# Two convolutions inside a recurrent block: ScalarE's taps given to VectorE and GpSimd, four accumulators instead of two

## The chip, the cores and the metric

The kernel runs on one core of a Trainium2 chip. The metric is device time in microseconds, the median of several runs.

## The reference

Two blocks of a network are computed on 256 tokens of width 1024, two layers each, batch 1, all in float32. The first block is the one that matters here. A layer projects the normed input `x` (and a context `ctx` of 256 tokens) to 2848 columns. The first 1024 go to a convolution branch: `val * sigmoid(gate)` gives 512 channels, and each channel is convolved along the 256 tokens with its own 31 weights, a bias is added, then a group norm over groups of 64 channels and SiLU follow:

```
def conformer_conv(u, conv_w, conv_b, cnorm_g, cnorm_b):
    val, gate = jnp.split(u, 2, axis=-1)
    z = val * jax.nn.sigmoid(gate)
    z = dwconv(z, conv_w) + conv_b
    z = group_norm(z, CONV_GROUPS, cnorm_g, cnorm_b, LN_EPS)
    return jax.nn.silu(z)
```

The other columns feed a recurrence (RWKV) over 8 heads of 64, forward and backward in time. Both branches are concatenated and projected; a gated feed-forward follows. The second layer of the context needs the recurrence alone. The second block (another mixer and four feed-forwards) has no such convolution.

## The kernel before

Activations lie with 128 features on the partitions and the 256 tokens along the free axis; 512 channels are four such tiles. Weights come from memory on SyncE's queue as tiles of 128 x 1024 (`raw`, four buffers); ScalarE makes a rounded high part `wh` (line 341) and VectorE the remainder `wl` (line 342), and TensorE does three products for each.

**The stages.** `first` (line 1412) runs four recurrences: on `ctx` of layer 0 ("wide", until some 330 us), on `x` of layer 0 ("half", from some 395 us on, beside the feed-forward of `ctx`), on `ctx` of layer 1 ("all", its inverse at some 840 to 910 us), and on `x` of layer 1 ("wide", some 1080 to 1350 us). A recurrence in chunks of 64 tokens needs the inverse of 32 x 32 triangular blocks (`inverse`, line 944): 31 steps of a product (962) and a difference (964) on VectorE, two block transpositions (967, 969), products on TensorE, and the assembly of two tiles `Q` of 128 x 1024. Each `Q` is set to zero on GpSimd (987), filled in part by copies on ScalarE and VectorE (995), and finished with negated products (1009 on ScalarE, 1011 on VectorE). Then `reads` (1014, masks at 1029), `values` (1041, masks at 1065) and `chain` (1075), which carries the state through four chunks in either direction, alternate TensorE with ScalarE and VectorE.

**The filler of a wide stage.** While the recurrence runs, other work is laid between: `conv_in` (line 659; the product with the sigmoid at 670 gives `z`), and the steps of `ada_steps` (478), which turn 512 KB tiles into modulation vectors through a copy on ScalarE (497, tile `T2b`). In the first wide stage the filler begins with loading and norming `x` (`then_x`, 1454), in both versions.

**The convolution** (`conv`, line 700) is traced behind the recurrence of a wide stage (1443), for each tile `f` of four in turn. The tap in the middle and the taps nearest to it are VectorE's: one instruction (726) multiplies the shifted `z` by its weight and adds to an accumulator `av` (tile `T1c`, two buffers), which 719 begins, behind the last step of the inverse by an explicit order. The farthest taps are GpSimd's: a product (732) into a buffer `tap` (two of them) and an addition (733) into the output `zc`, which 720 sets to zero. Those in between are ScalarE's: it makes the product (730) in the same two buffers, and GpSimd adds it. `NPOOL` and `NPOOLE` (line 38) give, for the first and second wide stage, how many of the 30 outer taps GpSimd and ScalarE take: 10 and 3, then 9 and 3, so VectorE keeps 17, then 18. Last, 737 on VectorE adds `av`, the bias and `zc`. A third convolution (`x` of layer 0, `NPOOLC`) has all taps on GpSimd, behind the first one in its queue, from about 244 to 541 us. Each ends in `group_norm` (745), whose squares also lie in `T1c`.

**The order.** The framework writes the order of each engine's instructions before the run, from the order of tracing as priority and a planned duration for each instruction; on the chip every engine follows its list, and an instruction that waits holds back all behind it. The convolution is traced last in its stage, so its taps are planned into times at which an engine has nothing earlier to do.

Of the kernel before, what the change touches and what calls it, by code (L numbers as in the profile page):

```python
# [12 lines left out]
ALU = mybir.AluOpType  # L13
# [21 lines left out]

NLAST = 2, 4

NPOOL, NPOOLE, NPOOLC = (10, 3), (9, 3), (30, 0)
NTAP = 2

QC, EVERY = (1,), 2
# [217 lines left out]
class Prog:  # L259
# [427 lines left out]
    def mixed_in(self, conv, y, perm=False):  # L687

        mix = self.mixtiles()
        for f in range(NF):  # L690
            src = (conv if f < 4 else y)[:, f % 4, :]
            if perm:
                t = self.T1([P, T])
                a, b = self.unperm(t, src, True)
                self.nc.gpsimd.tensor_copy(a, b)
                src = t
            self.split(src, *mix[f])
        return mix

    def conv(self, l, z, acc, npool, hold=False):  # L700


        nc = self.nc
        o = COLS[f"convw{l}"][0]
        taps = sorted((j for j in range(31) if j != 15), key=lambda j: abs(j - 15))
        nv, na = 30 - npool[0] - npool[1], npool[1]
        parts = [("v", taps[:nv]), ("a", taps[nv : nv + na]), ("p", taps[nv + na :])]

        order = []
        for k, js in parts:  # L710
            order += [((i + 0.5) / len(js), k, j) for i, j in enumerate(js)]
        order.sort()
        zc = [acc[:, f, :] for f in range(4)]
        for f in range(4):
            w = lambda j: self.cols[:, o + 4 * j + f : o + 4 * j + f + 1]
            av = self.T1([P, T]) if nv else None
            if nv:
                with self.tc.issue_after(self.inverted.ins):
                    nc.vector.tensor_scalar(av, z[:, f, :], w(15), None, ALU.mult)
                nc.gpsimd.memset(zc[f], 0.0)  # L720
            else:
                nc.gpsimd.tensor_scalar(zc[f], z[:, f, :], w(15), None, ALU.mult)
            for i, (_, k, j) in enumerate(order):
                d, s = slice(max(0, 15 - j), min(T, T + 15 - j)), slice(max(0, j - 15), min(T, T + j - 15))
                if k == "v":
                    nc.vector.scalar_tensor_tensor(av[:, d], z[:, f, s], w(j), av[:, d], ALU.mult, ALU.add)  # L726
                else:
                    t = self.t(self.pool, [P, T], "tap", bufs=NTAP)
                    if k == "a":
                        nc.scalar.mul(t[:, d], z[:, f, s], w(j))  # L730
                    else:
                        nc.gpsimd.tensor_scalar(t[:, d], z[:, f, s], w(j), None, ALU.mult)  # L732
                    nc.gpsimd.tensor_add(zc[f][:, d], zc[f][:, d], t[:, d])  # L733
                if i % 5 == 4:
                    yield
            if nv:
                nc.vector.scalar_tensor_tensor(zc[f], av, self.col(f"convb{l}", f), zc[f], ALU.add, ALU.add)
            else:
                nc.gpsimd.tensor_scalar(zc[f], zc[f], self.col(f"convb{l}", f), None, ALU.add)
            yield  # L740
        while hold and not self.go:
            yield
        self.group_norm(zc, f"cng{l}", f"cnb{l}", LN_EPS, AF.Silu)
# [200 lines left out]
    def inverse(self, Ld, Lo):  # L944

        nc = self.nc
        fl = lambda t: t.rearrange("p d a c x -> p (d a c) x")  # L950
        Ld, Lo = fl(Ld), fl(Lo)
        tj = self.S([P, 32, 32])
        nc.vector.transpose(tj.rearrange("p r c -> p c r"), Ld.rearrange("p j c -> p c j"))
        X = self.S([P, 32, 32])
        nc.gpsimd.memset(X, 0.0)
        xf = X.rearrange("p r c -> p (r c)")
        nc.gpsimd.memset(xf[:, 0:1024:33], 1.0)
        for k in range(31):
            m = 31 - k
            tmp = self.T1([P, 256])  # L960
            tv = tmp[:, 0 : m * (k + 1)].rearrange("p (a b) -> p a b", b=k + 1)
            nc.vector.tensor_mul(tv, tj[:, k + 1 : 32, k : k + 1].broadcast_to([P, m, k + 1]),  # L962
                                 X[:, k : k + 1, 0 : k + 1].broadcast_to([P, m, k + 1]))
            self.inverted = nc.vector.tensor_sub(X[:, k + 1 : 32, 0 : k + 1], X[:, k + 1 : 32, 0 : k + 1], tv)  # L964
        yield
        qt = self.S([P, 32, 32])
        nc.vector.transpose(qt, X)
        qc = self.S([P, 32, 32])
        nc.vector.transpose(qc, X.rearrange("p r c -> p c r"))

        zss = []
        for d in range(2):
            pz = self.ps((P, 16, 32))
            zs = Lo[:, 16 * d : 16 * d + 16, :]
            for j in range(16):
                J = 16 * d + j
                for h in range(2):
                    r = slice(64 * h + 32, 64 * h + 64)
                    w = slice(64 * h, 64 * h + 32)
                    self.mm(pz[w, j, :], Lo[r, J, :], qt[r, :, J], tile_position=(64 * h + 32, 64 * h))  # L980
            for h in range(2):
                w = slice(64 * h, 64 * h + 32)
                (nc.scalar.copy if h else nc.vector.tensor_copy)(zs[w], pz[w])
            zss.append(zs)
        Q = [self.S([P, 16, CH]) for _ in range(2)]
        for d in range(2):
            nc.gpsimd.memset(Q[d], 0.0)
            js = slice(16 * d, 16 * d + 16)
            src, zs = (qt, qc)[d], zss[d]
            po = self.ps((P, 16, 32))  # L990
            for q in range(4):
                s = slice(32 * q, 32 * q + 32)
                o = (q % 2) * 32
                dst, v = Q[d][s, :, o : o + 32], src[s][:, :, js].rearrange("p c j -> p j c")
                (nc.vector.tensor_copy if q % 2 else nc.scalar.copy)(dst, v)
            for j in range(16):
                J = 16 * d + j
                for h in range(2):
                    w = slice(64 * h, 64 * h + 32)
                    r = slice(64 * h + 32, 64 * h + 64)  # L1000
                    if d == 0:
                        self.mm(po[w, j, :], qc[w, :, J], zs[w, j, :], tile_position=(64 * h, 64 * h))
                    else:
                        self.mm(po[r, j, :], zs[w, j, :], qc[w, :, J], tile_position=(64 * h, 64 * h + 32))
            for h in range(2):
                w = slice(64 * h + 32 * d, 64 * h + 32 * d + 32)
                dst = Q[d][w, :, 32 * (1 - d) : 32 * (1 - d) + 32]
                if h:
                    nc.scalar.mul(dst, po[w], -1.0)
                else:  # L1010
                    nc.vector.tensor_scalar(dst, po[w], -1.0, None, ALU.mult)
        self.Q = Q
# [399 lines left out]
    def first(self):  # L1412
# [41 lines left out]
        def then_x():  # L1454

            zt = lambda: self.t(self.pool, [P, D], "z", bufs=2)
            early.append(self.norm1(0, self.load("x", [zt(), zt()]), 0, False, self.Sr, keep=True))
            yield
            early.append(z())
            mods, conv = self.ada_steps(0, (2, 3, 4, 5)), self.conv_in(0, *early)  # L1460
            for i, _ in enumerate(mods):
                yield
                if i % 4 == 1:
                    next(conv, None)
                    yield
            yield from conv
# [103 lines left out]

TAGS1 = {
    ("Sb", "t"): ("Sb", 2), ("S", "r"): ("S", NS), ("S", "t"): ("S", NS), ("S", "b"): ("Sb", 2),
# [3 lines left out]
    ("tiny", "r"): ("tn", 6), ("tiny", "b"): ("tnb", 4), ("tiny", "c"): ("tnc", 2),  # L1576
}
# [63 lines left out]
```

## Time and profile before

| | us |
|---|---|
| median of 3 runs | 2794.75 |
| lowest and highest | 2785.89, 2794.93 |
| the profiled execution, its own time | 2795.86 |
| its span, first to last instruction | 2794.10 |

The profile is of one execution. Its busy times and waits add up to its span, 1.76 us less than that execution took. Engines: PE is TensorE's matmul, PEld its weight load, DVE VectorE, ACT ScalarE, POOL GpSimd. A row of groups gives line, engine, operation, output and input, shape, count, busy time and mean of one, then the idle time before them and who ended it.

### The profile page before, as it was taken

The page shows a single profiled execution, that of the slowest core. Times are in us where ns is not written, and L with a number is a line of the kernel's source. Part 1 is how long each engine was busy: PE and PEld are TensorE (multiplying, and loading weights), DVE is VectorE, ACT ScalarE, POOL GpSimd, SP SyncE. Part 2 cuts the span into 40 slices and gives each one's busy share as a digit, 9 for nine tenths or more (in the row PEclk, how much of TensorE's full clock was granted, in tenths as well). Part 3 has the DMA queues.
Part 4 walks back from the last instruction along what each step waited for, and adds up shares of the span by engine and source line. Part 5 has one row for each costly group of instructions (what it writes and reads, how often), then busy time and mean ns, then how long its engine had stood idle before and what let it go on. Part 6 is the DMA issues. An engine that isn't in the chain of part 4 may idle for free.

```text
span 2794.1 us, 53718 instructions
## 1 busy us (share of the span) xinstructions
PE 2640.2 (94%) x22398; PEld 2307.3 (83%) x22398; DVE 1728.3 (62%) x2735; ACT 1318.7 (47%) x2007; POOL 613.7 (22%) x609
## 2 busy tenths in 40 slices
PE   7879988999989998989899899999999999999998
PEld 4867777888668897866699899889899898889897
DVE  3894678744578555895555655665655655755655
ACT  5532454433565346532544544554444544644543
POOL 0288899700130001391200000010000000100000
PEclk8978999999999999978899999999999999999999
DMA  7325433433423354234255555524555554525653
GB/s 249 103 75 186 163 129 129 152 135 131 166 76 107 123 180 159 94 127 170 101 186 184 200 187 184 193 91 149 176 188 184 186 184 166 177 90 181 203 184 118
DMA packets 118768, 430.71 MB, mean 154 GB/s; under 512 B 13174, under 2 KB 13686, under 8 KB 118524
## 3 DMA queue, kind: packets, MB, share of 16 engines
q1 hardware_dynamic: 118524, 427.28, 43.9%
q8 instruction: 175, 2.87, 0.4%
q14 instruction: 69, 0.57, 0.1%
HBM read 425.13 MB, written 2.10 MB: 153 GB/s over the span
## 4 chain that ended last, share of the span: by engine, by line
PE 78%; DVE 13%; ACT 4%; issue 2%; DMA 2%; POOL 1%; SPq 0%; ACTq 0%; DVEq 0%; POOLq 0%
PE pb L333 33%; PE acc L333 24%; PE ps L333 19%; DVE wl L342 2%; DVE T1c L726 2%; DVE S L964 1%; DVE T L962 1%; DMA raw<-in_ada 1%; ACT wh L341 1%; POOL tap L732 1%; DVE acc L619 0%; PE acc L438 0%; DVE x L620 0%; DMA raw<-in_wr 0%; DVE S L851 0%
## 5 line engine op out<-in xcount | busy, mean ns | idle before, releaser
L342 DVE TENSOR_TENSOR wl<-raw,wh 128x1024 fp32r<-128x1024 f32 (+1 forms) x654 | 809.7, 1241 | 628.6 <-ACT wh L341 395.1
L341 ACT CAST wh<-raw 128x1024 fp32r<-128x1024 f32 (+1 forms) x654 | 681.7, 1046 | 901.1 <-PE pb L333 343.7
L333 PE MATMUL pb<-xf,wh 128*128 128x256 f32 (+1 forms) x2560 | 489.7, 289 | 14.7 <-DVE T1b L588 4.3
L333 PE MATMUL pb<-S,wh 128*128 128x256 f32 x2560 | 496.4, 291 | 4.3 <-DVE S L630 2.6
L333 PEld LDWEIGHTS pb<-xf,wh 128*128 128x128 f32 (+1 forms) x2560 | 411.6, 195 | 29.7 <-DVE T1b L588 8.1
L333 PEld LDWEIGHTS pb<-S,wh 128*128 128x128 f32 x2560 | 413.4, 194 | 22.0 <-issue 9.8
L333 PE MATMUL ps<-S,wh 128*128 128x256 f32 x2048 | 392.4, 288 | 0.9 <-ACT S L460 0.8
L333 PE MATMUL pb<-xf,wl 128*128 128x256 f32 (+1 forms) x1280 | 371.8, 291 | 1.5 <-DVE wl L342 1.4
L333 PE MATMUL pb<-S,wl 128*128 128x256 f32 x1280 | 370.2, 289 | 0.4 <-DVE wl L342 0.4
L365 POOL TENSOR_TENSOR wl<-raw,wh 128x1024 fp32r<-128x1024 f32 x22 | 52.0, 2374 | 1392.7 <-ACT wh L364 1000.8
L333 PEld LDWEIGHTS ps<-S,wh 128*128 128x128 f32 x2048 | 328.4, 193 | 9.7 <-issue 3.4
L333 PE MATMUL ps<-S,wl 128*128 128x256 f32 x1024 | 294.1, 287 | 1.8 <-DVE wl L342 1.8
L333 PEld LDWEIGHTS pb<-xf,wl 128*128 128x128 f32 (+1 forms) x1280 | 249.0, 194 | 8.0 <-DVE wl L342 2.9
L333 PEld LDWEIGHTS pb<-S,wl 128*128 128x128 f32 x1280 | 248.6, 194 | 5.2 <-issue 3.3
L333 PE MATMUL acc<-wh,T 128*128 128x512 f32 x704 | 206.3, 393 | 0.0
L333 PEld LDWEIGHTS ps<-S,wl 128*128 128x128 f32 x1024 | 197.3, 193 | 3.8 <-DVE wl L342 2.0
L333 PE MATMUL acc<-wh,T1b 128*128 128x512 f32 x528 | 159.0, 399 | 3.5 <-ACT T1b L341 3.5
L333 PEld LDWEIGHTS acc<-wh,T 128*128 128x128 f32 x704 | 127.0, 189 | 23.6
L732 POOL TENSOR_SCALAR tap<-z,cols 128x255 f32<-128x255 f32 (+14 forms) x120 | 138.2, 1161 | 0.0
L333 PEld LDWEIGHTS acc<-wh,T1b 128*128 128x128 f32 x528 | 95.1, 190 | 22.4 <-ACT T1b L341 4.4
L333 PE MATMUL acc<-wl,T 128*128 128x512 f32 x352 | 113.2, 395 | 0.0
L733 POOL TENSOR_TENSOR z<-z,tap 128x255 f32<-128x255 f32 (+14 forms) x120 | 110.4, 920 | 4.1
(444 smaller groups left out, 3949.4 us busy)
## 6 DMA issues: line engine op xcount, KB each, us to landing
raw<-in_fu SPq DMA_DIRECT2D x132, 512.0 KB, 3.2
raw<-in_ada SPq DMA_DIRECT2D x96, 512.0 KB, 4.2
raw<-in_pu SPq DMA_DIRECT2D x88, 512.0 KB, 4.3
raw<-in_qu SPq DMA_DIRECT2D x88, 512.0 KB, 4.0
raw<-in_fd SPq DMA_DIRECT2D x66, 512.0 KB, 3.2
raw<-in_wr SPq DMA_DIRECT2D x51, 512.0 KB, 4.2
raw<-in_pd SPq DMA_DIRECT2D x44, 512.0 KB, 4.3
raw<-in_qd SPq DMA_DIRECT2D x44, 512.0 KB, 3.3
```

The costliest lines, as they stand in the source:

```text
L333: return self.nc.tensor.matmul(out, lhsT, rhs, start=start, stop=stop, **kw)
L341: self.nc.scalar.copy(hi, src)
L342: self.nc.vector.tensor_sub(lo, src, hi.bitcast(F32))
L365: self.nc.gpsimd.tensor_sub(lo, r, hi.bitcast(F32))
L726: nc.vector.scalar_tensor_tensor(av[:, d], z[:, f, s], w(j), av[:, d], ALU.mult, ALU.add)
L732: nc.gpsimd.tensor_scalar(t[:, d], z[:, f, s], w(j), None, ALU.mult)
L733: nc.gpsimd.tensor_add(zc[f][:, d], zc[f][:, d], t[:, d])
L962: nc.vector.tensor_mul(tv, tj[:, k + 1 : 32, k : k + 1].broadcast_to([P, m, k + 1]), X[:, k : k + 1, 0 : k + 1].broadcast_to([P, m, k + 1]))
L964: self.inverted = nc.vector.tensor_sub(X[:, k + 1 : 32, 0 : k + 1], X[:, k + 1 : 32, 0 : k + 1], tv)
```

## The change

The counts of taps become 11 for GpSimd and 0 for ScalarE in both wide stages, so VectorE has 19. The bias is added where the accumulator begins (719), and the accumulator is added to GpSimd's sum by GpSimd (line 737's place). `T1c` has four buffers instead of two, and `T2b` one instead of two. The zeros of `Q` in `inverse`, in all four recurrences, are written by VectorE.

```diff
--- before.py
+++ after.py
@@ -35,7 +35,7 @@
 
 NLAST = 2, 4
 
-NPOOL, NPOOLE, NPOOLC = (10, 3), (9, 3), (30, 0)
+NPOOL, NPOOLE, NPOOLC = (11, 0), (11, 0), (30, 0)
 NTAP = 2
 
 QC, EVERY = (1,), 2
@@ -716,7 +716,7 @@
             av = self.T1([P, T]) if nv else None
             if nv:
                 with self.tc.issue_after(self.inverted.ins):
-                    nc.vector.tensor_scalar(av, z[:, f, :], w(15), None, ALU.mult)
+                    nc.vector.tensor_scalar(av, z[:, f, :], w(15), self.col(f"convb{l}", f), ALU.mult, ALU.add)
                 nc.gpsimd.memset(zc[f], 0.0)
             else:
                 nc.gpsimd.tensor_scalar(zc[f], z[:, f, :], w(15), None, ALU.mult)
@@ -734,7 +734,7 @@
                 if i % 5 == 4:
                     yield
             if nv:
-                nc.vector.scalar_tensor_tensor(zc[f], av, self.col(f"convb{l}", f), zc[f], ALU.add, ALU.add)
+                nc.gpsimd.tensor_add(zc[f], zc[f], av)
             else:
                 nc.gpsimd.tensor_scalar(zc[f], zc[f], self.col(f"convb{l}", f), None, ALU.add)
             yield
@@ -984,7 +984,7 @@
             zss.append(zs)
         Q = [self.S([P, 16, CH]) for _ in range(2)]
         for d in range(2):
-            nc.gpsimd.memset(Q[d], 0.0)
+            nc.vector.memset(Q[d], 0.0)
             js = slice(16 * d, 16 * d + 16)
             src, zs = (qt, qc)[d], zss[d]
             po = self.ps((P, 16, 32))
@@ -1570,8 +1570,8 @@
 
 TAGS1 = {
     ("Sb", "t"): ("Sb", 2), ("S", "r"): ("S", NS), ("S", "t"): ("S", NS), ("S", "b"): ("Sb", 2),
-    ("T1", "r"): ("T1", 4), ("T1", "b"): ("T1b", 6), ("T1", "c"): ("T1c", 2),
-    ("T2", "r"): ("T2", 3), ("T2", "t"): ("T2", 3), ("T2", "b"): ("T2b", 2),
+    ("T1", "r"): ("T1", 4), ("T1", "b"): ("T1b", 6), ("T1", "c"): ("T1c", 4),
+    ("T2", "r"): ("T2", 3), ("T2", "t"): ("T2", 3), ("T2", "b"): ("T2b", 1),
     ("tD", "r"): ("tD", 2), ("tD", "b"): ("tDb", 2),
     ("tiny", "r"): ("tn", 6), ("tiny", "b"): ("tnb", 4), ("tiny", "c"): ("tnc", 2),
 }
```

## Rows read from the trace of the kernel before

**Rows 1.** The page, part 1: busy time of each engine over the span.
```profile
PE 2640.2 (94%) x22398; PEld 2307.3 (83%) x22398; DVE 1728.3 (62%) x2735; ACT 1318.7 (47%) x2007; POOL 613.7 (22%) x609
```

**Rows 2.** Busy time by stretch; columns: stretch, its us, busy (x instructions), PEclk, DMA.
```profile
164.00:228.00 64.00, 54.25 (x692) 44.48 (x692) 60.35 (x122) 23.93 (x44) 53.11 (x53) 0.61 0.23 83
228.00:290.00 62.00, 61.19 (x732) 44.13 (x731) 21.77 (x43) 14.93 (x26) 53.45 (x62) 0.93 0.66 233
1208.00:1268.00 60.00, 48.80 (x616) 35.19 (x616) 59.04 (x113) 17.67 (x30) 53.66 (x57) 0.63 0.33 123
1268.00:1333.00 65.00, 64.55 (x823) 42.29 (x820) 29.50 (x76) 18.97 (x37) 2.46 (x4) 0.92 0.43 155
```

**Rows 3.** Chain of waits, 1100 to 1350 us; columns: start, us, what.
```profile
1245.24 6.73 DVE T1c L726 x11
```

**Rows 4.** Groups by line, VectorE, 164 to 229 us; busy and mean ns, then idle before.
```profile
L726 DVE SCALAR_TENSOR_TENSOR T1c<-x,cols,T1c 128x255 f32<-128x255 f32 (+8 forms) x68 | 35.1, 558 | 0.2
L719 DVE TENSOR_SCALAR T1c<-x,cols 128x256 f32<-128x256 f32 x4 | 2.1, 576 | 0.0
L737 DVE SCALAR_TENSOR_TENSOR x<-T1c,cols,x 128x256 f32<-128x256 f32 x3 | 2.0, 691 | 0.0
```

**Rows 5.** Groups by line, VectorE, 1208 to 1268 us.
```profile
L726 DVE SCALAR_TENSOR_TENSOR T1c<-x,cols,T1c 128x255 f32<-128x255 f32 (+8 forms) x72 | 41.3, 628 | 0.1
L737 DVE SCALAR_TENSOR_TENSOR x<-T1c,cols,x 128x256 f32<-128x256 f32 x3 | 1.4, 466 | 0.0
```

**Rows 6.** Page, part 5: the weight split on VectorE.
```profile
L342 DVE TENSOR_TENSOR wl<-raw,wh 128x1024 fp32r<-128x1024 f32 (+1 forms) x654 | 809.7, 1241 | 628.6 <-ACT wh L341 395.1
```

**Rows 7.** Timeline of VectorE, first wide stage; columns: start, us, then what.
```profile
166.53 1.23 DVE L967 STREAM_TRANSPOSE S<-S 128x1024 f32<-128x1024 f32 x1
182.91 2.23 DVE L726 SCALAR_TENSOR_TENSOR T1c<-x,cols,T1c 128x252 f32<-128x252 f32 x5
186.84 2.09 DVE L995 COPY S<-S 32x512 f32<-32x512 f32 x2 [1.69 <-POOL S L987]
197.09 0.68 DVE L1011 TENSOR_SCALAR S<-ps 32x512 f32<-32x512 f32 x1
200.87 1.53 DVE L737 SCALAR_TENSOR_TENSOR x<-T1c,cols,x 128x256 f32<-128x256 f32 x2
```

**Rows 8.** Timeline of VectorE, second wide stage.
```profile
1215.65 1.23 DVE L967 STREAM_TRANSPOSE S<-S 128x1024 f32<-128x1024 f32 x1
1227.99 2.37 DVE L726 SCALAR_TENSOR_TENSOR T1c<-x,cols,T1c 128x250 f32<-128x250 f32 x4
1241.10 0.68 DVE L1011 TENSOR_SCALAR S<-acc 32x512 f32<-32x512 f32 x1
```

**Rows 9.** Groups by line, GpSimd, 164 to 229 us.
```profile
L732 POOL TENSOR_SCALAR tap<-x,cols 128x243 f32<-128x243 f32 (+4 forms) x21 | 27.0, 1294 | 0.0
L733 POOL TENSOR_TENSOR x<-x,tap 128x244 f32<-128x244 f32 (+6 forms) x28 | 24.3, 867 | 8.8 <-ACT tap L730 7.5
```

**Rows 10.** Groups by line, ScalarE, whole span.
```profile
L730 ACT ACTIVATE tap<-x,cols 128x246 f32<-128x246 f32 (+2 forms) x24 | 12.0, 502 | 41.4 <-POOL x L733 39.2 <-DVE x L670 2.2
L497 ACT COPY T2b<-pb 128x512 f32<-128x512 f32 x20 | 11.7, 584 | 31.5 <-PE pb L333 31.3
```

**Rows 11.** Busy time by stretch, around the third inverse.
```profile
510.00:545.00 35.00, 34.36 (x506) 32.07 (x506) 23.23 (x32) 17.02 (x22) 33.35 (x34) 0.85 0.38 125
```

**Rows 12.** Timeline of VectorE, the inverse beside the feed-forward.
```profile
509.93 1.23 DVE L967 STREAM_TRANSPOSE S<-S 128x1024 f32<-128x1024 f32 x1
524.56 0.68 DVE L1011 TENSOR_SCALAR S<-ps 32x512 f32<-32x512 f32 x1 [0.93 <-PE ps L333]
```

**Rows 13.** Timeline of GpSimd: first tap, and a later idle time.
```profile
133.57 1.86 POOL L732 TENSOR_SCALAR tap<-x,cols 128x245 f32<-128x245 f32 x2 [24.37 <-DVE x L670]
...
272.69 0.93 POOL L722 TENSOR_SCALAR z<-z,cols 128x256 f32<-128x256 f32 x1 [3.38 <-DVE z L670]
```

**Rows 14.** Timeline of VectorE, where it waits for GpSimd.
```profile
455.21 0.42 DVE L962 TENSOR_TENSOR T<-S,S 128x31 f32<-128x31 f32 x1 [3.14 <-POOL S L957]
```

## The prediction

> **What bounds the kernel now.** I began with the busy time of each engine. TensorE is busy for 94% of the span [rows 1], so a change to the vector engines counts only where TensorE waits. The next view, busy time in equal slices, sent me to the two wide stages, and busy time by stretch shows them side by side. From the end of each inverse, VectorE is full, 60.4 of 64 us and 59.0 of 60, while TensorE's granted clock is 0.61 and 0.63 and ScalarE is busy for 23.9 and 17.7 us. Right behind, VectorE is down to 21.8 of 62 and 29.5 of 65 us, TensorE is full and its clock 0.92 to 0.93 [rows 2]. The chain of waits in the second stretch goes through VectorE's taps, 6.7 us of them in one piece [rows 3]. So in two stretches, 124 us together, the time is the sum of VectorE's list, and the taps fill 35.1 and 41.3 us of it [rows 4, 5]. Elsewhere TensorE decides. The view to settle the sum in is therefore VectorE's groups in these stretches.
>
> **The change, part by part.** A term is positive where it makes the kernel longer.
>
> *Taps.* VectorE goes from 17 to 19 per tile in the first wide stage (8 more) and from 18 to 19 in the second (4 more). One takes 35.1/68 = 0.516 us and 41.3/72 = 0.574 us of VectorE [rows 4, 5]: 8 x 0.516 = 4.1 and 4 x 0.574 = 2.3, **+6.4**.
>
> *Sums.* VectorE's last additions go to GpSimd; three of four lay in each stretch, 2.0 and 1.4 us [rows 4, 5]: **-3.4**. The fourth of each lies behind the stretch, where VectorE has room. The bias moves into an instruction that is there anyway: 0.
>
> *Four accumulators.* 719 never stands idle waiting for its buffer: 0.0 [rows 4]. Two at a time already keep VectorE full, so 0 here.
>
> *Zeros of Q.* The trace has no zeroing on VectorE. From below, 719 covers a quarter of the width in 2.1/4 = 0.53 us [rows 4]; from above, the weight split covers the same 128 x 1024 with two inputs in 1.24 us [rows 6]. I take 1.1, near the row of the same shape; four fall into the two stretches, **+4.4** (2.1 to 5.0).
> The Trainium skill (VectorE: DVE Perf Modes, Zero memsets can be issued as uint32) has a memset at one cycle per element whatever the type; an estimate from that, 1024 elements at VectorE's 0.96 GHz, is 1.07 us, and no row here shows it. With it the term would be 4.3.
>
> *The wait for the zeros.* At 186.84 us VectorE stands idle for 1.69 us until GpSimd has zeroed Q behind its own taps [rows 7]: **-1.7**. Ahead of that copy VectorE's list has five taps, 2.23 us, and four, 2.37 us, in the second wide stage [rows 7, 8]; I read them as put there because Q was not ready. With the zeros in VectorE's own list the copy can follow the transpositions, and these taps run later, at best where VectorE has room. That is worth 0 to -4.6; I take **-4.6**, since the stretch behind is 60% idle on VectorE [rows 2].
>
> *GpSimd without ScalarE's taps.* In the first stretch GpSimd waits 7.5 us for ScalarE's products [rows 9]. This is now work, and it slows VectorE: where GpSimd is busy for 53.7 of 60 us instead of 53.1 of 64 [rows 2], a tap costs 0.574 - 0.516 = 0.058 more. For the 7.5/0.516 = 15 taps beside it that is **+0.9** (0 to 1.8).
> The Trainium skill (SBUF — State Buffer, Who interferes with whom) says more: VectorE with two inputs in SBUF and GpSimd reading it exclude each other for a whole instruction, while ScalarE has ports of its own. That rule speaks against the change: 24 products leave the port that nobody shares. Taken whole, each of the 12 new taps on VectorE could wait a full GpSimd addition of 24.3/28 = 0.87 us [rows 9], 10.4 us in place of the 6.4 above, and the sum would be +6.0. The rows agree in direction alone: taps cost more where GpSimd is busier.
>
> *ScalarE.* It loses 24 products, 12.0 us, and 39.2 us of standing still for GpSimd's buffers [rows 10]. I cost this at 0, the striking number of the page notwithstanding: behind it work waits, but VectorE's list is full at the same time. The most it can give is what VectorE is idle in the stretches beyond the 1.7 counted, 3.65 + 0.96 - 1.7 = 2.9 [rows 2]. If VectorE's cover went, ScalarE's waits would come next.
>
> *The other two inverses.* Four zeros there too, at 0: beside the feed-forward TensorE is busy for 34.4 of 35 us [rows 11]. Without that cover, 4 x 1.24 = 5.0 more; 0 to gain, as nothing of TensorE's idle time is there to win beyond 0.6.
>
> *T2b with one buffer.* The 20 copies wait for TensorE's products, 31.3 us, not for a buffer [rows 10]. TensorE reads a copy before it makes what the next one waits for, so 0; no gain is possible.
>
> *GpSimd's list.* No DMA is issued in what moves, and SyncE's queue is passed by nothing. On GpSimd the two wide stages have 23 and 21 tap instructions per tile before, 22 and 22 after and one sum. The sum waits for VectorE, and behind it stand the taps of the next tiles and the third convolution; this is the second rival.
>
> Sum: 6.4 - 3.4 + 4.4 - 1.7 - 4.6 + 0.9 = **+2.0 us**. The profiled execution took 2795.86 us (span 2794.10 and 1.76 around it), 1.1 above the median shown; against the median I forecast 2794.75 + 2.0 = **2796.8 us**. With all bounds one way: no taps displaced +4.6, zeros +0.6, other inverses +5.0, port +0.9, together 2808; the other way zeros -2.3, ScalarE -2.9, port -0.9, inverses -0.6, together 2790. I count 0.5%, 14 us, as what a measurement can tell from no change, so this case lies within it.
>
> **Rivals.** *The inverse's tail gets free (faster).* From the first transposition to the last negated product it takes 166.53 to 197.77, 31.2 us, and 1215.65 to 1241.78, 26.1 us, with taps between [rows 7, 8]; beside the feed-forward, without taps, 509.93 to 525.24, 15.3 us [rows 12]. If Q that is ready sooner takes not nine taps but most of them out of these tails, and they end behind the stretch, half of the excess is 7.9 + 5.4 = 13.3 us and the whole 26.7; I put this case at -20, **2777 us**. For it: low clock and idle TensorE beside a full VectorE [rows 2]. Against it: taps put off still have to run, and the masks that the recurrence waits for stand in the same list. It decides where more than some 25 taps (25 x 0.55 = 14 us) leave the stretches.
>
> *GpSimd waits for VectorE at the sum (slower).* GpSimd begins at 133.57 us [rows 13]; with 11 products and 11 additions and the sum, a tile takes 11 x 1.29 + 12 x 0.87 = 24.6 us [rows 9], so two are through at 183. VectorE ends the first two accumulators at about 200.87 us [rows 7]. If the list has the sums right behind each tile's taps, GpSimd stands still for some 18 us; with four accumulators in turn, longer. A lag of 3.4 us is lost again where GpSimd waits for z of the third convolution [rows 13]; the rest stays, as that convolution alone has 4 x 30 x 2 = 240 instructions for GpSimd, and in the "half" stage VectorE already waits 3.1 us for GpSimd's zeros of the inverse [rows 14]. So 18 - 3.4, about 15 us: **2812 us**. Against it: GpSimd gains 7.5 us in the same place, and a planned order may put the sums later. It decides when GpSimd's lag at the end of the first wide stage is over 3.4 us.
>
> *The change does little of what it says.* Accumulators that nobody waited for and a ScalarE that nobody waited for would leave the time as it is: that is inside the forecast, at 2795.
>
> **How the numbers follow.** The forecast's case, all terms small, 0.52, with its own range 2790 to 2808. The free tail 0.27: the engine lists are written anew, and 124 us of half-used TensorE is much to win. GpSimd's wait 0.21. The range reaches from 2771, into most of the first rival, to 2816, just past the second. Faster by over 0.5% takes the first rival alone, slower the second.
>
> **What would show it.** Right: VectorE still full in both stretches, their length within 4 us, 76 taps in each at 0.5 to 0.6 us, zeros at about 1.1 us followed at once by the copies, ScalarE without the 39 us and no shorter stage for it. First rival: taps seen behind the stretch, tails under 25 us. Second: GpSimd idle at its sums until VectorE is done, and the waits at the "half" inverse grown. Wrong altogether: a difference of over 10 us in a part without convolution or inverse.

## The result, and the profile after

The changed kernel takes **2805.98 us**, the median of 5 runs (2800.15 to 2811.6), against 2794.39 for the kernel before in the same comparison, 11.6 us more. The ratio over all executions is **1.0052**, 95% interval 1.0029 to 1.0075, half a per cent longer. That lies at the edge of what the prediction called no change, inside the range of its likeliest case. The profiled execution took 2805.98 us with a span of 2804.2, 10.1 us more than before.

The page's busy times of the changed kernel hardly differ from before [rows 1]:

```profile
PE 2641.4 (94%) x22398; PEld 2304.8 (82%) x22398; DVE 1731.0 (62%) x2747; ACT 1309.6 (47%) x1983; POOL 614.5 (22%) x609
```

The busy time by stretch, with the bounds of [rows 2]:

```profile
164.00:228.00 64.00, 52.83 (x661) 42.83 (x661) 63.28 (x124) 21.68 (x38) 59.96 (x56) 0.63 0.22 83
228.00:290.00 62.00, 59.01 (x662) 42.09 (x662) 21.47 (x42) 12.76 (x22) 49.25 (x59) 0.89 0.59 206
1208.00:1268.00 60.00, 53.81 (x616) 33.57 (x615) 55.29 (x114) 15.08 (x24) 53.33 (x55) 0.69 0.34 121
1268.00:1333.00 65.00, 58.30 (x842) 40.32 (x842) 30.07 (x78) 15.62 (x32) 14.40 (x18) 0.92 0.51 182
```

VectorE (the third busy time) is fuller in the first taps' stretch, but in the second it now stands idle for 4.7 of 60 us, where it was full. Its groups, first stretch (164 to 234 us), to be read against [rows 4]:

```profile
L726 DVE SCALAR_TENSOR_TENSOR T1c<-x,cols,T1c 128x255 f32<-128x255 f32 (+9 forms) x76 | 42.1, 599 | 0.1
L987 DVE MEMSET S<- 128x1024 f32 x2 | 1.8, 912 | 0.3 <-issue 0.2 <-DVE T1c L726 0.2
```

And in the second (1208 to 1275 us), against [rows 5]:

```profile
L726 DVE SCALAR_TENSOR_TENSOR T1c<-x,cols,T1c 128x255 f32<-128x255 f32 (+9 forms) x76 | 37.4, 544 | 0.1
L987 DVE MEMSET S<- 128x1024 f32 x2 | 1.8, 912 | 0.3 <-DVE T1c L726 0.2 <-issue 0.2
```

So 76 taps in each, 0.554 and 0.492 us of VectorE apiece, and zeros whose records last 0.91 us. Where the zeros stand shows in the timeline of VectorE in the second wide stage (start, us, then what):

```profile
1220.11 1.23 DVE L967 STREAM_TRANSPOSE S<-S 128x1024 f32<-128x1024 f32 x1
...
1236.05 0.42 DVE L1065 TENSOR_TENSOR T<-acc,const 64x256 f32<-64x256 f32 x1 [1.71 <-PE acc L333]
1236.39 1.94 DVE L969 STREAM_TRANSPOSE S<-S 128x1024 f32<-128x1024 f32 x1
...
1240.10 0.91 DVE L987 MEMSET S<- 128x1024 f32 x1 [0.16 <-DVE T1c L726]
1240.94 1.52 DVE L726 SCALAR_TENSOR_TENSOR T1c<-x,cols,T1c 128x252 f32<-128x252 f32 x4
1242.49 2.01 DVE L995 COPY S<-S 32x512 f32<-32x512 f32 x2
...
1255.23 0.68 DVE L1011 TENSOR_SCALAR S<-acc 32x512 f32<-32x512 f32 x1
```

The inverse's tail, from 967 to the end of the last 1011, is 35.8 us, before 26.1 [rows 8]. Four taps stand between a zero and the copies that need it, and VectorE waits for TensorE in the middle of it.

**Where the time went.** I cut both executions at the transposition of `Ld` (953) that opens a wide stage, and at the first product with the gate (619) behind it:

| stretch | before | after | difference |
|---|---|---|---|
| start to 953 of the first wide stage | 110.9 | 113.9 | +3.0 |
| first wide stage, 953 to 619 | 287.2 | 291.2 | +4.0 |
| to 953 of the second | 762.8 | 761.6 | -1.2 |
| second wide stage, 953 to 619 | 201.6 | 207.4 | +5.8 |
| the rest of the span | 1431.5 | 1430.1 | -1.4 |

The first line is no effect of the change: up to there both programs have the same order of instructions. Each column is one execution: two more executions with the list of the kernel before (in part 2 below, where only the second stage differs) took 763.4 and 757.1 us where 762.8 stands here, so a difference of a few us in one line is not shown by it. The second wide stage, cut at 953, 967, the last 1011, the group norm of the recurrence (385) and 619, looks so before and after (columns as in [rows 2]):

```profile
1160.94:1215.65 54.71, 48.33 (x534) 39.58 (x533) 52.55 (x109) 18.92 (x32) 35.11 (x37) 0.95 0.35 126
1215.65:1241.78 26.13, 25.70 (x403) 19.28 (x403) 25.36 (x48) 11.15 (x17) 21.07 (x21) 0.63 0.39 142
1241.78:1326.16 84.38, 76.07 (x988) 52.48 (x984) 50.96 (x116) 22.06 (x42) 26.28 (x29) 0.83 0.41 151
1326.16:1362.58 36.42, 35.87 (x133) 24.18 (x133) 21.28 (x35) 16.23 (x26) 10.51 (x12) 0.91 0.26 93
```

```profile
1166.67:1220.11 53.44, 43.36 (x513) 38.08 (x513) 50.96 (x105) 16.39 (x26) 33.28 (x35) 0.96 0.33 120
1220.11:1255.91 35.80, 35.80 (x428) 21.61 (x430) 31.49 (x60) 10.40 (x15) 35.17 (x34) 0.69 0.31 108
1255.91:1335.92 80.01, 73.31 (x983) 50.15 (x981) 43.28 (x110) 20.15 (x38) 20.60 (x25) 0.87 0.45 164
1335.92:1374.12 38.20, 37.32 (x133) 25.37 (x133) 20.36 (x35) 16.12 (x26) 7.39 (x12) 0.87 0.26 86
```

The tail grew by 9.7 us and what is behind it lost 4.4. TensorE (first busy time) has no gap in the tail at all, at a granted clock of 0.69, between its levels of 1.2 (0.5) and 2.4 GHz (1.0), and does 428 products there instead of 403.

The prediction read the chain of waits in one piece [rows 3]. By line, over the whole second wide stage, before and after, it is:

```profile
by line: PE acc L333 29.9%; PE pb L333 15.4%; DVE T1c L726 12.3%; PE ps L333 6.5%; DVE S L964 5.5%; DVE T L962 5.2%; DVE wl L342 5.2%; issue 2.9%; DVE S L1029 2.4%; DMA raw<-in_ada 2.1%; DVE T L1065 1.3%; DVE S L953 1.1%; ACT S L995 1.0%; D
```

```profile
by line: PE acc L333 34.7%; PE pb L333 18.5%; PE ps L333 7.8%; DVE T L962 5.4%; DVE wl L342 5.2%; DVE S L964 4.9%; DVE T1c L726 3.8%; DMA raw<-in_ada 2.9%; issue 2.7%; DVE S L1029 2.3%; DMA raw<-in_wo 1.6%; PE acc L1052 1.4%; DVE S L953 1.1
```

VectorE's taps (`DVE T1c L726`) hold 12.3% of 201.6 us, 24.8, before and 3.8% of 207.4, 7.9, after; TensorE's products (`PE`) took their place. In the first wide stage it went the other way, 7.4% of 287.2 us, 21.3, before and 12.2% of 291.2, 35.5, after:

```profile
by line: PE pb L333 36.9%; PE acc L333 16.2%; DVE T1c L726 7.4%; PE ps L333 6.7%; DVE T L962 3.5%; DVE wl L342 3.3%; POOL tap L732 3.3%; DVE S L964 3.2%; issue 2.6%; DMA raw<-in_wc 1.8%; POOL x L733 1.5%; DMA z<-in_x 1.4%; DVE S L995 1.3%; 
```

```profile
by line: PE pb L333 35.3%; PE acc L333 16.3%; DVE T1c L726 12.2%; PE ps L333 7.5%; DVE wl L342 3.9%; DVE T L962 2.9%; issue 2.5%; DVE S L964 2.5%; DVE T L1065 1.6%; DMA raw<-in_wc 1.5%; DMA z<-in_x 1.3%; DVE S L995 1.1%; DVE xf L342 1.0%; D
```

### The profile page after: what moved, and what is told of

It reads as the page before. It is cut to its first block, busy times and chain, and to the rows that moved or that the text cites. A ratio compares the mean times of both kernels' runs of the same rounds, so it can differ in the third digit from the quotient of the medians.

```text
span 2804.2 us, 53671 instructions
## 1 busy us (share of the span) xinstructions
PE 2641.4 (94%) x22398; PEld 2304.8 (82%) x22398; DVE 1731.0 (62%) x2747; ACT 1309.6 (47%) x1983; POOL 614.5 (22%) x609
## 4 chain that ended last, share of the span: by engine, by line
PE 78%; DVE 14%; ACT 4%; DMA 2%; issue 2%; POOL 0%; SPq 0%; ACTq 0%; DVEq 0%; POOLq 0%
PE pb L333 33%; PE acc L333 25%; PE ps L333 19%; DVE wl L342 3%; DVE T1c L726 2%; DVE T L962 1%; DVE S L964 1%; PE acc L438 1%; DMA raw<-in_ada 1%; ACT wh L341 1%; DVE acc L619 0%; DMA raw<-in_wr 0%; DVE x L620 0%; DVE tDb L519 0%; ACT L384 0%
## 5 line engine op out<-in xcount | busy, mean ns | idle before, releaser
L732 POOL TENSOR_SCALAR tap<-x,cols 128x245 f32<-128x245 f32 (+5 forms) x88 | 101.0, 1158 | 46.8 <-DVE x L670 46.8
```

## The experiments

The theories: **load**, the one of the prediction (the time is VectorE's work in the two stretches); **tail**, in the first expectations called order theory (taps that stand between transposition and last negated product make the tail long); **GpSimd** (sums wait for VectorE); and, formed after the first four runs, **filler** (the modulation steps: the 64 products with `csil` on 32 loads of 512 KB that TensorE's list spreads over the second wide stage).

**1. Undo one part, or move the taps.** Zeros back on GpSimd:

```diff
-            nc.vector.memset(Q[d], 0.0)
+            nc.gpsimd.memset(Q[d], 0.0)
```

> The changed kernel with the zeros of Q back on GpSimd. Load theory (what counts is how much work VectorE's list has in the two stretches): four zeros of 0.91 us leave the stretches, 2806 - 3.6 = 2802 us. Order theory (what counts is how many taps the planned order puts between the first transposition and the last negated product of a wide inverse): the list has 27 and 35 taps there, the changed kernel's 29 and 36, so 3 x 0.55 = 1.7 less, 2804 us. GpSimd theory (sums wait for VectorE): 2806 us, or more, since GpSimd gets four zeros behind its taps again. The three lie close together; what tells is the tail of the second inverse: 35 us or more by the order theory, under 33 by the load theory.

Two accumulators and two `T2b` again:

```diff
-    ("T1", "r"): ("T1", 4), ("T1", "b"): ("T1b", 6), ("T1", "c"): ("T1c", 4),
-    ("T2", "r"): ("T2", 3), ("T2", "t"): ("T2", 3), ("T2", "b"): ("T2b", 1),
+    ("T1", "r"): ("T1", 4), ("T1", "b"): ("T1b", 6), ("T1", "c"): ("T1c", 2),
+    ("T2", "r"): ("T2", 3), ("T2", "t"): ("T2", 3), ("T2", "b"): ("T2b", 2),
```

> The changed kernel with two accumulators T1c (and two T2b) as before; taps, sums and zeros stay as changed. Load theory: VectorE has the same work, 2805 to 2807 us. Order theory: the list has 19 and 28 taps between the first transposition and the last negated product in place of 29 and 36, 18 fewer: 18 x 0.55 = 10 us less, 2796 us, and the second tail some 31 us in place of 35.8. GpSimd theory: with two accumulators the sums of the first two tiles come earlier, a few us less, 2802 us, with the tail as long as it is.

The kernel before with line 987 alone changed:

```diff
-            nc.gpsimd.memset(Q[d], 0.0)
+            nc.vector.memset(Q[d], 0.0)
```

> The kernel before with only the zeros of Q moved to VectorE. Load theory: 4 x 0.91 us more in the stretches, less the wait of 1.69 us for GpSimd: 2794.4 + 2 = 2796.5 us. Order theory: the list has 23 and 21 taps in the tails, the kernel before 28 and 27: 11 fewer, 6 us less, 2788 us or a little more for the zeros, 2790; both tails under 30 and 26 us.

The changed kernel with no tap in a tail (719 is ordered behind what `self.inverted` names):

```diff
-                    nc.vector.tensor_scalar(dst, po[w], -1.0, None, ALU.mult)
+                    self.inverted = nc.vector.tensor_scalar(dst, po[w], -1.0, None, ALU.mult)
```

> The changed kernel with the accumulators' begin ordered behind the last negated product of the inverse, so that no tap stands in the two tails. Load theory: the same work in another order, and VectorE's taps still have to end before the group norm: 2804 to 2808 us. Order theory: the tails of 32.0 and 35.8 us fall to some 17 us each (15.3 beside the feed-forward, without taps); the taps run in the stretch behind, where VectorE is idle for some 40 and 35 us and TensorE is full: 2806 - 15 - 19 = 2772 us at best, and 2785 if half of it comes back where the third convolution or the group norm waits.

Measured, as ratio to the kernel before (2791.9 us in that comparison): zeros back **0.9943** (0.9920 to 0.9965), median 2777.2 us; two accumulators 1.0039 (1.0025 to 1.0054); zeros alone 1.0006 (0.9995 to 1.0017); taps behind 1.0042 (1.0028 to 1.0057). The load theory had three of the four: 2805 to 2807 us with two accumulators (2805.2 came), 2 us more for the zeros alone (1.7 by the ratio), 2804 to 2808 with the taps behind (2804.9). It missed the zeros back by 25 us: to take four zeros of some 1 us in the two stretches, and four elsewhere, away from VectorE gave 29 us, where to add them to the kernel before cost nothing that can be told. The tail theory missed all four; with all taps out of the tails the time stayed. The second wide stage of that last run, tail and the piece behind:

```profile
1208.71:1239.52 30.81, 28.99 (x429) 22.94 (x430) 14.23 (x24) 11.42 (x17) 30.10 (x37) 0.61 0.17 59
1239.52:1339.26 99.74, 89.94 (x991) 60.43 (x987) 63.91 (x155) 20.08 (x38) 24.32 (x28) 0.71 0.45 159
```

VectorE is busy for 14.23 of 30.81 us, and the tail still takes 30.8: neither the taps nor a full VectorE set the length of this tail. The piece behind takes 99.7 us, where the run with the zeros back needs 61.9:

```profile
1219.95:1251.61 31.66, 31.27 (x433) 20.69 (x434) 29.28 (x58) 9.46 (x14) 23.09 (x26) 0.76 0.51 177
1251.61:1313.47 61.86, 60.47 (x958) 42.29 (x951) 43.38 (x106) 19.59 (x37) 28.42 (x32) 0.98 0.48 172
```

Besides the taps, which add to VectorE's work in that piece (63.91 and 43.38 us), two differences stand out: the granted clock behind the inverse (0.71, 0.98; before 0.83), and how much has been loaded by then (59 and 177 GB/s in the tail). The loads are those of the modulation steps: TensorE's list leaves 52 of their 64 products behind the inverse with the taps behind, 48 with two accumulators, 41 in the changed kernel, 40 before and with the zeros alone, 34 with the zeros back. That is the order of the second stage's lengths: 216.5, 208.6, 207.4, 201.6 and 203.3, 186.8 us. What goes with a lower clock shows in one group of TensorE behind the inverse, the same 128 products of the chain in the kernel before, with the zeros back and with the taps behind, in this order:

```profile
L333 PE MATMUL ps<-S,xf 128*64 128x64 f32 x128 | 7.7, 235 | 0.0
```

```profile
L333 PE MATMUL ps<-S,xf 128*64 128x64 f32 x128 | 6.6, 223 | 0.0
```

```profile
L333 PE MATMUL ps<-S,xf 128*64 128x64 f32 x128 | 9.8, 274 | 0.0
```

**2. Move the modulation steps, leave VectorE's work as it is.** In `rwkv` the filler of the second wide stage is traced ahead of the rest of the inverse, and so gets its priority (the call moves the steps of `conv_in` too):

```diff
-        for _ in inv:
+        for _ in (wide and l and fill(24)) or inv:
             pass
         Q = self.Q
```

It was put into the changed kernel, the kernel before, and the changed kernel with the zeros on GpSimd; in the last run (kernel before) the same call stands at `tok = []`, ahead of `reads` and `values`.

> The changed kernel, traced so that in the second wide stage the modulation steps come ahead of the rest of the inverse; taps, sums, zeros and accumulators as changed. New theory (filler theory: the stage's length follows how many of its 64 modulation products TensorE's list leaves behind the last product of the inverse; so far, products behind and us from L953 to L619: 34 and 186.8, 40 and 201.6 and 203.3, 41 and 207.4, 48 and 208.5, 52 and 216.5, some 1.5 us each): 28 behind in place of 41, 13 x 1.5 = 20 us less, 2786 us. Load theory (VectorE's work in the two stretches): the same work, 2804 to 2808 us. Tail theory (taps ahead of the last negated product): 33 taps in the second tail in place of 36, 2 us less, 2804 us.

> The kernel before with the same move of the modulation steps, nothing of the change. Filler theory: 20 products behind the inverse in place of 40, 20 x 1.5 = 30 us less, 2764 us, or some 2775 if the products now ahead hold up the inverse. Load theory: no change, 2792 us. Tail theory: VectorE's list has 49 taps in the second tail in place of 27, 22 x 0.57 = 12 us more, 2804 us.

> The changed kernel with the zeros of Q on GpSimd (which ran at 2777 us with 34 products behind) and the same move of the modulation steps. Filler theory: 24 behind in place of 34, 15 us less, 2762 us, or near 2770 if the gain levels off. Load theory: 2777 us. Tail theory: 42 taps in the second tail in place of 35, 4 us more, 2781 us.

> The kernel before with the modulation steps traced right behind the 31 steps of the inverse, ahead of the read and value products: no product is left behind the inverse in TensorE's list. Filler theory: 40 x 1.5 = 60 us less could not be, since their loads take time of their own (16.8 MB at some 300 GB/s is 56 us): the inverse is held up by them, so between 2765 and 2790 us, with the second tail over 40 us. Load theory: 2792 us. Tail theory: 51 taps in the tail in place of 27, 14 us more, 2806 us.

Measured: changed kernel 2792.1 us, 0.9999 (0.9987 to 1.0011), 14 us less with all its VectorE and GpSimd work in place; kernel before 2779.0, **0.9948** (0.9931 to 0.9966), 13 us less; zeros back 2781.7, 0.9955 (0.9937 to 0.9973), no further gain; all ahead 2792.8, 1.0002 (0.9985 to 1.0018). The load theory, which had no change for the first two, is refuted as an account of the time, and so is the tail theory: the kernel before gained with a tail that grew from 26.1 to 41.3 us. But the move helps both kernels alike: with it the changed kernel is still 13 us slower than the kernel before, about as much as without it. So it is a gain of its own, and does not show what the change's loss comes from. Rows of the kernel before with the move, tail and the piece behind:

```profile
1214.98:1256.28 41.30, 38.24 (x512) 23.14 (x510) 38.37 (x78) 14.24 (x24) 34.13 (x30) 0.79 0.54 191
1256.28:1313.27 56.99, 54.14 (x882) 40.10 (x882) 35.25 (x88) 18.20 (x36) 15.97 (x20) 0.95 0.43 150
```

The filler theory had the sign of the first two but sizes too large (20 us for 14, and 30, or 17 if the products now ahead held up the inverse, for 13), and it missed the third: the count of products behind is not a law. With none behind, the tail took 50.1 us and the clock fell behind the inverse instead, to 0.74 over 57.6 us.

**3. The parts alone, on the kernel before, and a combination.** The taps:

```diff
-NPOOL, NPOOLE, NPOOLC = (10, 3), (9, 3), (30, 0)
+NPOOL, NPOOLE, NPOOLC = (11, 0), (11, 0), (30, 0)
```

> The kernel before with only the counts of taps changed (11 and 0 in both stages). Load theory, by the prediction's term: 4.1 us more in the first wide stage and 2.3 in the second, 2792 + 6.4 = 2798 us. Filler theory: TensorE's list leaves 48 modulation products behind the second inverse in place of 40, as in the run with two accumulators, whose second stage took 208.5 us against 201.6: 7 us more there and nothing in the first, 2799 us. The totals agree; the stages tell: L953 to L619 of the first 291 us or 287, of the second 204 or 208.

The sums and the bias, lines 719 and 737 as in the change (here the second):

```diff
-                nc.vector.scalar_tensor_tensor(zc[f], av, self.col(f"convb{l}", f), zc[f], ALU.add, ALU.add)
+                nc.gpsimd.tensor_add(zc[f], zc[f], av)
```

> The kernel before with only the sums on GpSimd and the bias in the accumulator's begin. Load theory, by the prediction's term: 3.4 us less, 2788.5 us. Filler theory: 40 products behind the inverse as before, 2792 us. GpSimd theory: sums that wait for VectorE, up to 3 us more, 2795 us.

The buffers, the two lines of `TAGS1` shown above the other way round:

```diff
-    ("T1", "r"): ("T1", 4), ("T1", "b"): ("T1b", 6), ("T1", "c"): ("T1c", 2),
-    ("T2", "r"): ("T2", 3), ("T2", "t"): ("T2", 3), ("T2", "b"): ("T2b", 2),
+    ("T1", "r"): ("T1", 4), ("T1", "b"): ("T1b", 6), ("T1", "c"): ("T1c", 4),
+    ("T2", "r"): ("T2", 3), ("T2", "t"): ("T2", 3), ("T2", "b"): ("T2b", 1),
```

> The kernel before with only four accumulators (and one T2b). Load theory, by the prediction's term: the same, 2792 us. Filler theory: 39 products behind the inverse in place of 40 and the last of them 184 rows behind it in place of 225, 2788 to 2792 us. Tail theory: 31 and 31 taps in the two tails in place of 28 and 27, 4 us more, 2796 us.

The combination is the changed kernel with two accumulators and two `T2b` and the diff of part 2:

> The changed kernel with two accumulators and two T2b, and with the modulation steps traced ahead of the rest of the second wide stage's inverse. Filler theory: 32 products behind the inverse in place of 48, the second stage some 192 us in place of the 208.5 of the run without that move, 2805 - 15 = 2790 us; less if the 284 us of that run's first stage hold, which are 3 less than the kernel before has. Load theory: as the run without the move, 2805 us. Tail theory: 24 taps in the second tail in place of 28, 2803 us.

Measured: taps alone 1.0013 (1.0000 to 1.0025), sums alone **0.9972** (0.9960 to 0.9983), four accumulators (with one `T2b`) alone **0.9977** (0.9965 to 0.9988), the combination 0.9998 (0.9989 to 1.0008). With zeros alone (1.0006), the four parts add up to +0.13 - 0.28 - 0.23 + 0.06 = -0.32%, and together they make +0.52%. The stages tell more than the totals: taps alone is 5.7 us shorter in the first, with eight taps more, and 13.6 longer in the second. That is neither theory's split; the filler theory has the sign of the second alone. The load theory's -3.4 for the sums and 0 for the accumulators lie outside what was measured, and the GpSimd theory had the sums' sign wrong. For the combination (2793.2 us) the second stage came to 200.1 us, 8.5 shorter than without the move where 16 were expected.

The profiled executions, us. "Behind": modulation products that TensorE's list leaves behind the second inverse. The last three columns split the second wide stage: from its busy times in steps of 4 us, "work" is TensorE's busy time times the granted clock, summed; "clock" is its busy time less that; "idle" is the rest. The work should be equal in all; it scatters by 5 either way, which is the error of this split.

| kernel | behind | first stage | second stage | work | clock | idle |
|---|---|---|---|---|---|---|
| before | 40 | 287.2 | 201.6 | 158 | 28 | 16 |
| after | 41 | 291.2 | 207.4 | 163 | 27 | 18 |
| zeros back | 34 | 291.9 | 186.8 | 161 | 15 | 11 |
| two accumulators | 48 | 284.2 | 208.6 | 159 | 28 | 22 |
| zeros alone | 40 | 287.5 | 203.3 | 158 | 28 | 18 |
| taps behind | 52 | 284.2 | 216.5 | 155 | 45 | 17 |
| after, early | 28 | 288.2 | 194.9 | 164 | 17 | 14 |
| before, early | 20 | 286.8 | 191.4 | 159 | 18 | 14 |
| zeros back, early | 24 | 288.5 | 191.0 | 165 | 15 | 11 |
| before, all early | 0 | 287.0 | 206.7 | 165 | 31 | 10 |
| taps alone | 48 | 281.5 | 215.2 | 161 | 32 | 23 |
| sums alone | 40 | 276.5 | 199.1 | 160 | 23 | 16 |
| four accumulators alone | 39 | 279.6 | 194.2 | 161 | 15 | 19 |
| two accumulators, early | 32 | 288.1 | 200.1 | 162 | 26 | 11 |

Each row is one execution. The profiled execution with two accumulators (2792.2 us) was 13 us below the median of its runs, so its row is on the short side; the other variants' were within some 5 us of theirs. The three kernels with the same order in the first stage (before, before early, before all early) agree there within 0.4 us.

## Why the prediction was right or wrong

**The time was in the range, its first step was wrong.** 2796.8 us was forecast and 2806 came, inside 2790 to 2808; the sum had +2.0 and +11.6 was measured. The step on which the sum stood, "in two stretches, 124 us together, the time is the sum of VectorE's list", failed. In the second wide stage the taps run from 1208.8 to 1266.1 us before and from 1216.2 to 1272.6 after: 0.9 us shorter, and 17 us less of the chain of waits is theirs, in a stage that is 5.8 longer. And in part 2 the time moved by 13 and 14 us with VectorE's work unchanged. The second stage is instead, in each of 14 kernels, some 160 us of TensorE's work at full clock, plus what it stands idle, plus what it loses to a lower clock; this split says where the time lies and not what causes it. That TensorE is idle or slow beside a full VectorE did not make VectorE the bound. In the first stage, where the chain holds 14 us more of taps and the time is 4.0 longer, the step is not refuted. So it is luck that the range held: its bounds were made of terms of a sum that did not set the time. Of the prediction's own signs, the 76 taps and the end of ScalarE's 39 us came; VectorE was not full in the second stretch, and the copies did not follow the zeros at once.

**What the parts also did is rewrite the order.** That the order counts is shown: the same operations in another list gained 0.5% on the changed kernel and on the kernel before, by a move of the filler. That the change's own loss runs through the place of the modulation steps is not shown, since the two kernels lie about as far apart with the move (2792.1 and 2779.0 us) as without it; that the loss comes from the order at all is argued, from 29 us for the zeros and from parts that do not add. In the table's last columns most of the two gains (28 to 18 before, 27 to 17 after) are clock; in the combination the gain is idle time (22 to 11). That the clock rises because these products lie beside the inverse's small ones is argued from those rows, not tried by itself; the combination, with 24 of them in the tail and a clock of 0.58 there, speaks against a simple rule.

**Terms.** *Taps +6.4*: VectorE's taps grew from 76.4 to 79.5 us, +3.1; alone they cost 3.6 us (0.0 to 7.0), but as -5.7 and +13.6 in the two stages, so the agreement of the sum is chance. *Sums -3.4*: alone -7.8 (-11.2 to -4.7); its first stage is 10.7 us shorter, where VectorE was spared 2.0. *Four accumulators 0*: with one `T2b`, alone -6.4 (-9.8 to -3.4); no run has one without the other. Nobody waited for a buffer, as the prediction said, yet the framework could lay out the list otherwise.

*Zeros +4.4*: right, two in a row start 1.07 us apart, so some 4.3. With *the wait for the zeros -1.7* and *the displaced taps -4.6* the prediction had -1.9; alone it measured +1.7 (-1.4 to +4.7). The displaced taps are the part that failed. With the zeros alone, 23 and 21 taps stand in the tails where 28 and 27 did, eleven gone where nine were counted, and the time did not fall; in the changed kernel 29 and 36 stand there, and the zeros were laid among them. The copies of ScalarE wait longer for them, over the whole span, than they did for GpSimd's; before, then after with the group of `T2b`:

```profile
L995 ACT COPY S<-S 32x512 f32<-32x512 f32 x16 | 17.5, 1092 | 7.6 <-POOL S L987 7.5
```

```profile
L995 ACT COPY S<-S 32x512 f32<-32x512 f32 x16 | 17.6, 1098 | 12.7 <-DVE S L987 12.6
L497 ACT COPY T2b<-pb 128x512 f32<-128x512 f32 x20 | 11.7, 585 | 40.1 <-PE pb L333 40.0
```

*T2b 0*: right, 497 still waits for TensorE alone. *ScalarE 0*: not contradicted, its 24 products and 39 us of standing still went and no tail is shorter (32.0 and 35.8 us after, 31.2 and 26.1 before); no run takes them away by themselves. *The other two inverses 0*: right, 0.6 and 0.3 us longer from 967 to the last 1011.

*GpSimd's density +0.9*: in the first stretch a tap cost 0.038 more with GpSimd busy for 60.0 of 64 us, in the second 0.082 less with it as busy as before. Tap by tap the trace says more. Of 140 taps before, 15 have no GpSimd instruction beside them: 0.465 us on average, none over 0.479. The other 125 take 0.609 on average and up to 0.990, though half of them no more than 0.483. After, 29 take 0.460 and 123 take 0.598. So a tap beside GpSimd is dearer by 0.14 us, but the change put no more of them there: 0 in place of +0.9. The Trainium skill (SBUF — State Buffer, Who interferes with whom) has such a tap and a GpSimd instruction that reads SBUF exclude each other; the trace agrees in direction, with half of the taps beside GpSimd no longer than those alone.

**Rivals.** *The inverse's tail gets free* did not come, and with no tap in them the tails still take 28.2 and 30.8 us, at an unchanged time of the kernel. *GpSimd waits for VectorE at the sum* came as a wait and not as a loss. GpSimd's sums in the second stage, 1208 to 1290 us:

```profile
L737 POOL TENSOR_TENSOR x<-x,T1c 128x256 f32<-128x256 f32 x4 | 3.6, 904 | 8.9 <-DVE T1c L726 8.8
```

GpSimd was through at 1285.7 us, and the convolution's group norm first read the sums at 1329.4. In the first stage it waited 2.0 us there and then 2.5 for `z` of the third convolution, so no lag was left.

**What stays open.** Why the change costs 12 to 13 us, with the moved filler and without it, is not shown. Nor is the changed kernel's +4.0 in its first wide stage: it lies behind the inverse (119.3 us to the group norm, 111.6 before), and the parts alone for taps, sums and accumulators are all shorter there than before. No run moved the filler of that stage. Nor is the +5.8 of the second split further: clock and idle time differ by less than the split's error.

## What to carry to other kernels

Where a framework writes each engine's list, judge a change by the stage's binding engine first: its busy time times granted clock, against the stage's length, says the most there is to win, and a full second engine beside a half-idle first one says little. An edit of some 4 us moved the time by 29 here, and parts did not add, so measure the combination, and steer the order of the filler itself. When such a move is meant to explain a loss, put it into both kernels and compare those. Three versions here are fastest, too close to be told apart: the changed kernel with the zeros of `Q` left on GpSimd (0.9943), the kernel before with its modulation steps traced ahead of the rest of the inverse (0.9948), and the first of these with the same move (0.9955). They came from experiments and not from the sum.

## What the runs showed that was not expected

TensorE's granted clock was 0.5 (1.2 GHz) in stretches in which its records leave no gap: in the changed kernel it is busy for all of 35.80 us in the second tail at a mean of 0.69, with 428 products, most of them small. A piece of it, and the piece just ahead, at 1.0:

```profile
1232.44:1242.68 10.24, 10.24 (x58) 5.15 (x57) 8.20 (x17) 3.21 (x5) 10.08 (x9) 0.50 0.33 118
1225.62:1232.44 6.82, 6.82 (x155) 5.37 (x154) 4.87 (x11) 1.06 (x2) 6.74 (x7) 1.00 0.47 156
```

So a busy share of 100% was no sign of full speed. The ends of products are modelled in these records, so gaps shorter than a product would not show in them. The Trainium skill (TensorE: Matmul & The Clock Gate, HAM oscillation — how this bites in real kernels) tells of a TensorE that falls back at waits for loads; here the lower clock stands in rows without such a gap.

The record of a zero of 128 x 1024 floats on VectorE lasts 0.912 us, eight times alike, but each has 0.16 to 0.17 us of idle time ahead of it, and where two follow each other they start 1.07 us apart:

```profile
518.63 0.91 DVE L987 MEMSET S<- 128x1024 f32 x1 [0.17 <-issue]
519.70 0.91 DVE L987 MEMSET S<- 128x1024 f32 x1 [0.16 <-issue]
```

The prediction's estimate of 1.07 us from the Trainium skill (VectorE: DVE Perf Modes, Zero memsets can be issued as uint32), one element per cycle, agrees with that distance, and not with the length of the record. What an instruction costs its engine is read from start to start.
